# Raw weights of a half-size tile loaded in two halves with buffers of their own, and no sums issued behind the last plain tile

## The chip, the core and the metric

The kernel runs on one core of a Trainium2 chip. Such a core has TensorE (PE) for matmuls, VectorE (DVE), ScalarE (ACT), GpSimd (POOL) and SyncE (SP), each with its own stream of instructions, and 16 DMA engines that all queues share. Here SP issues the loads of weights and POOL issues transfers between two places in DRAM. The metric is the time of one execution in microseconds of device time.

## The reference

One layer of a streaming encoder over 512 positions of 1024 features, in float32: a half-weighted SwiGLU block (FFN1), a mixer (chunked attention beside a pooling mixer), another SwiGLU block (FFN2), and a last norm.

```python
D_MODEL = 1024
SEQ = 512
D_FF = 2816

def rmsnorm(x, g):
    xf = x.astype(jnp.float32)
    y = xf * lax.rsqrt(jnp.mean(xf * xf, axis=-1, keepdims=True) + EPS)
    return (y * g.astype(jnp.float32)).astype(x.dtype)

def swiglu_ffn(x, w_gate, w_up, w_down):
    return (jax.nn.silu(x @ w_gate) * (x @ w_up)) @ w_down

x = x + 0.5 * swiglu_ffn(rmsnorm(x, ffn1_norm[l]), ffn1_w_gate[l], ffn1_w_up[l], ffn1_w_down[l])
x = x + hybrid_mixer(rmsnorm(x, mix_norm[l]), w_in[l], q_norm[l], k_norm[l], rel_bias[l],
                     pool_w[l], pool_scale[l], w_out[l])
x = x + 0.5 * swiglu_ffn(rmsnorm(x, ffn2_norm[l]), ffn2_w_gate[l], ffn2_w_up[l], ffn2_w_down[l])
x = rmsnorm(x, final_norm[l])
```

The change touches the two SwiGLU blocks alone.

## The kernel before

**Precision.** Every float32 operand is split in two parts, a high one (a cast on ACT) and a low one (the raw value less the high part, on DVE). A product of two operands is three matmuls, high by high, low by high and high by low (lines 192 to 194). So a weight panel can be used once it is loaded ("raw"), cast (`whi`) and subtracted (`wlo`).

**The up stage of a SwiGLU block.** The 2816 hidden features are 22 tiles of 128. A tile has a gate and an up panel of 1024x128 weights, loaded as 128x1024. Tiles 0 and 1 run together in four steps; tiles 2, 3 and 4 are "plain" (`PLAIN = 5`): each panel is loaded, split and multiplied over 8 blocks of 128 rows by 512 columns. The 17 tiles from 5 on are "half-size": the products of gate and up are worked out from seven products of half the size (in Winograd's manner), each of 12 matmuls by 256 columns, from blocks of the weights and sums of blocks.

**A half-size tile's weights.** The two panels make four blocks of 512 columns: up low (called 11), gate low, gate high, up high. Block 11 is split by `high11` and `low11`, the last two together by `high(22)` and `low(22)`. `sum13` makes the sums 11 + gate low and gate low + gate high (1024 columns in one instruction), `sum24` makes two more from these, and `high13`, `low13`, `high24`, `low24` split the sums. All of this for tile n+1 is done while the products of tile n run. In the trace all splits of blocks are lines 490 (ACT) and 495 (DVE), `sum13` is line 513 and `sum24` lines 519 and 520; evacuations by ACT are line 587.

**Raw buffers.** The four blocks of a tile lie in one buffer of 128x2048, of which there are two. `fetch(n)` issues two loads of 512 KB on SP: line 482 (gate low and gate high) and line 483 (up low and up high). `fetch(n + 2)` is called in tile n behind its second product and waits for `low(22)` of tile n, the last reader of the buffer. Sums and the down stage's panels use other buffers of 128x1024 (pool `weights`, also called raw).

**The down stage.** 42 products, seven kinds for each of six groups of the hidden features; most have 12 matmuls of 512 columns. Kinds A11, A12, S1 to S4 and A22 of the activations meet weights B11 to B22 or the sums T1 to T4 of these. The sums are made in DRAM by POOL while the up stage runs: `make_sums` pops a number from the list `RATES`, and issues so many steps (line 724), each a copy or an accumulating copy of 512 KB, behind a small copy (`mark`, line 722) of something that was just computed, which sets their time. T1 to T4 of group g are two steps each (T3-4-1 is the second, accumulating step of T3, group 4). What isn't done by the end of the up stage follows in the first products of the down stage. The panels (line 748) are fetched a few products ahead, in buffers that cycle through a list called `rooms`.

**What sets the order.** In the half-size tiles the order of PE, DVE, ACT and SP is that of the code. In the plain tiles a scheduler sets it. POOL's order is that of the code in `make_sums`. In the down stage of FFN2, SP also issues loads of the residual (`xt`, line 810) and of the last norm's gain.

Of the kernel before, what the change touches and what calls it, by code (L numbers as in the profile page):

```python
# [8 lines left out]
F32 = mybir.dt.float32  # L9
# [3 lines left out]
ALU = mybir.AluOpType  # L13
# [3 lines left out]
P = 128  # L17
D = 1024
S = 512
KD = D // P  # L20
NT = S // P
FF = 2816
KF = FF // P
# [15 lines left out]
ROOM, AHEAD_OF_PARTS, ALIGN = 1024 + 128, 16, 64  # L39
OFF, OFF_AT = (0, 2, 6), 32  # L40
PLAIN = 5
RATES = [3, 3, 2] + [1] * (PLAIN - 3) + [2] * (FF // P - PLAIN - 2) + [0] * 2
PROBS = 3
M_TILES = 16

# [24 lines left out]
def layer(  # L70
# [47 lines left out]
    def name(what):  # L118
        n_tiles[0] += 1
        return f"{what}_{n_tiles[0]}"  # L120
# [307 lines left out]
    def ffn_up(norm, wA, down, loaded):  # L428
# [45 lines left out]

        raws, w = {}, {}

        def fetch(n):

            if n < KF:
                f = down.order[n]  # L480
                raw = raws[n] = down.pool.tile([P, 4 * S], F32, tag="raw", name=name("raw"), bufs=RAW)
                nc.sync.dma_start(raw[:, S : 3 * S], wA[2 * f])
                nc.sync.dma_start(
                    raw.rearrange("p (b c) -> p b c", c=S)[:, 0:4:3],
                    wA[2 * f + 1].rearrange("p (b c) -> p b c", c=S),
                )

        def high(n, what, src, at=AHEAD_OF_PARTS):
            hi, lo = (z[:, : src.shape[-1]] for z in part_tiles(at))
            nc.scalar.copy(hi, src)  # L490
            w[what] = hi, lo, src
# [8 lines left out]

        def high11(n):
            if n < KF:
                high(n, (n, 11), raws[n][:, :S])

        def low11(n):
            if n < KF:
# [2 lines left out]
        def sum13(n):  # L509
            if n < KF:  # L510
                z = w[n, "odd"] = new_sum()
                raw = raws[n]
                nc.vector.tensor_tensor(z, raw[:, : 2 * S], raw[:, S : 3 * S], op=ALU.add)  # L513

        def sum24(n):
            if n < KF:
                z = w[n, "even"] = new_sum()
                raw, odd = raws[n], w[n, "odd"]
                nc.vector.tensor_tensor(z[:, :S], odd[:, :S], raw[:, 2 * S : 3 * S], op=ALU.add)
                nc.vector.tensor_tensor(z[:, S:], z[:, :S], raw[:, 3 * S :], op=ALU.add)  # L520

        def high13(n):
            if n < KF:
                off = n - PLAIN in OFF
                high(n, (n, 13), w[n, "odd"], OFF_AT if off else AHEAD_OF_PARTS)
# [27 lines left out]
        n, f = PLAIN - 1, down.order[PLAIN - 1]  # L553
        wj = [weights(wA[2 * f + j]) for j in range(2)]
        banks = [bank(), bank()]
        fetch(PLAIN)
        for k in range(KD):
            for j in range(2):
                mm3(banks[j], cut(wj[j], k * P, P), norm.h[k], k == 0, k == KD - 1)
            if k == 1:  # L560
                high11(PLAIN)
                low11(PLAIN)
                piece()
            elif k == 3:
                fetch(PLAIN + 1)
                sum13(PLAIN)
                high13(PLAIN)
                low13(PLAIN)
                piece()
            elif k == 5:  # L570
                sum24(PLAIN)
                piece()
# [22 lines left out]
        with tc.manual_schedule(engines={E.PE, E.DVE, E.Activation, E.SP}):  # L595
            last_silu = last_place = last_sums = nothing
            for n in range(PLAIN, KF):
                f = down.order[n]
                acc, up_lo, up_hi = bank()[:, :HT], bank()[:, :HT], abank()[:, :HT]
                u, z, sg = temp(), temp(), temp()  # L600
                w11, w13, w24 = (w[n, i][:2] for i in (11, 13, 24))
                product(acc, w11, A11, True)
                last_silu()
                last_place()
                high(n, (n, 22), raws[n][:, 2 * S :])
                low((n, 22))
                w22 = w[n, 22][:2]
                copy(u[:, :HT], acc)
                product(up_hi, cut(w13, S, S), S3, True)
                if n + 2 < KF:  # L610
                    fetch(n + 2)
                elif n + 2 == KF:

                    rooms[:] = [(down.pool, "raw", RAW, 4 * S)] * RAW
                    rooms.extend([(wpool, "raw", RAW, 1024)] * RAW)
                    n_raw[0] = 0
                    down.fetch(T2, 0)
                else:
                    down.fetch(B11, 0)
                    down.fetch(T1, 0)  # L620
                high11(n + 1)
                low11(n + 1)
                if n + 1 == KF:
                    down.pairs[S2, 0] = down.tokens(S2, 0)
                last_sums()
                sum13(n + 1)
                copy(z[:, HT:], up_hi, -1.0)
                product(acc, cut(w24, 0, S), S2, False)
                copy(u[:, HT:], acc, -1.0)
                sum24(n + 1)  # L630
                product(up_hi, cut(w24, S, S), A22, False)
                nc.vector.tensor_tensor(u[:, HT:], up_hi, u[:, HT:], op=ALU.add)  # L632
                down.make_sums(u[:, HT:], 2)
                product(acc, cut(w13, 0, S), S1, False)
                copy(z[:, :HT], acc)
                nc.vector.tensor_tensor(z[:, HT:], z[:, :HT], z[:, HT:], op=ALU.add)
                if n + 1 == KF:
                    down.parts[T2, 0] = down.weights(T2, 0)
                    down.pairs[A11, 0] = down.tokens(A11, 0)
                high13(n + 1)  # L640
                low13(n + 1)
                high24(n + 1)
                product(up_lo, cut(w22, S, S), A12, True)
                nc.scalar.activation(sg[:, HT:], z[:, HT:], AF.Silu)
                nc.vector.tensor_tensor(u[:, :HT], up_lo, u[:, :HT], op=ALU.add)
                low24(n + 1)
                if n + 1 == KF:
                    down.parts[B11, 0] = down.weights(B11, 0)
                product(acc, cut(w22, 0, S), S4, False)

                def last_silu(acc=acc, sg=sg):
                    nc.scalar.activation(sg[:, :HT], acc, AF.Silu, scale=-1.0)

                def last_place(f=f, u=u, sg=sg):
                    down.place(f, u, sg)

                def last_sums(f=f):
                    down.sums(f)

            last_silu()  # L660
            last_place()
            last_sums()
# [4 lines left out]
    class Down:  # L667
# [37 lines left out]
        def begin(self, pool):  # L705
            self.pool, self.acts = pool, []
            self.raws, self.parts, self.pairs = {}, {}, {}
            self.n_products, self.loads, self.loads_from = 0, [], 4
            self.open(range(G - 3))
            rooms[:] = [(wpool, "raw", RAW, 1024), (pool, "raw", RAW, 4 * S)] * RAW  # L710
            part_rooms[:] = [(wpool, HILO)] * HILO + [(pool, 1)]

        def rows(self, i, g):
# [1019 lines left out]
```

## Time and profile before

| | |
|---|---|
| median of 3 runs | 841.92 us (841.59 to 842.51) |
| profiled execution | 840.54 us, of which span 838.6 us |
| granted TensorE clock | 0.998 |
| busy share of PE, DVE, ACT, POOL | 99%, 85%, 60%, 16% |
| moved by DMA | 158.50 MB, mean 189 GB/s |

A row of the timeline is start, duration (both us), engine, line, operation, output<-inputs, shape, count, and in brackets how long the engine idled before and what ended that. A row of the chain is start, duration, what. PE's instructions are pipelined, so its durations overlap; the distance from one start to the next tells more. FFN1's half-size tiles begin near 62 us, FFN2's near 560 us, and FFN2's down stage near 724 us. `raw<-in_wA_dram` are loads of the up stage's weights, `raw<-in_wB_dram` and `raw<-wsum` of the down stage's panels and sums, `wsum<-in_wB_dram` and `wsum<-wsum` POOL's steps for the sums.

### The profile page before, as it was taken

How to read it: one execution, taken by the hardware profiler on the slowest of the kernel's cores; microseconds unless marked ns; L12 is line 12 of the kernel's file. 1: busy time of each engine (PE TensorE's matmuls, PEld its weight loads, DVE VectorE, ACT ScalarE, POOL GpSimd, SP SyncE). 2: the span in 40 equal slices, each digit the busy share in tenths (PEclk: the TensorE clock that was granted, in tenths of full speed). 3: DMA queues.
4: the chain of work that ended last, by engine and by line, in shares of the span. 5: the costliest groups of instructions: out<-in, count | busy, mean ns of one | idle time of the engine just before them, and what ended most of it. 6: DMA issues, size and time to landing. Idle time of an engine off the chain costs nothing.

```text
span 838.6 us, 14134 instructions
## 1 busy us (share of the span) xinstructions
PE 828.4 (99%) x5288; PEld 742.3 (89%) x5288; DVE 710.9 (85%) x1122; ACT 501.5 (60%) x859; POOL 132.7 (16%) x208
## 2 busy tenths in 40 slices
PE   9999999999999999999999999999999999999996
PEld 7889999999988888887888888889999999978885
DVE  7999998999897769767879678979989999878896
ACT  8446555665675656558748646355566555756573
POOL 0222122211053000102020000311121111132000
PEclk9999999999999999999999999999999999999999
DMA  8687887797499964322222117658887787689832
GB/s 291 160 228 201 215 210 212 209 231 197 151 269 290 304 210 132 113 88 89 75 76 76 51 55 271 195 132 222 239 208 194 206 226 202 251 265 344 261 110 100
DMA packets 72244, 158.50 MB, mean 189 GB/s; under 512 B 6112, under 2 KB 29168, under 8 KB 71792
## 3 DMA queue, kind: packets, MB, share of 16 engines
q1 hardware_dynamic: 49088, 110.93, 38.8%
q0 software_dynamic: 22656, 46.14, 26.1%
q8 instruction: 41, 0.67, 0.3%
q10 hardware_dynamic: 432, 0.54, 0.2%
q14 instruction: 27, 0.22, 0.1%
HBM read 153.38 MB, written 50.34 MB: 243 GB/s over the span
## 4 chain that ended last, share of the span: by engine, by line
PE 93%; DMA 4%; DVE 2%; ACT 1%; issue 0%; SPq 0%; ACTq 0%; DVEq 0%
PE mm L192 22%; PE mm L194 22%; PE mm L193 22%; PE a L192 7%; PE a L194 7%; PE a L193 7%; DMA raw<-in_wA_dram 2%; DMA raw<-in_wB_dram 1%; PE a L1293 1%; PE a L1229 1%; PE a L1281 1%; DVE wlo L495 1%; PE a L229 0%; PE a L1500 0%; PE a L1151 0%; DVE ha L149 0%
## 5 line engine op out<-in xcount | busy, mean ns | idle before, releaser
L149 DVE TENSOR_TENSOR wlo<-raw,whi 128x1024 fp32r<-128x1024 f32 (+2 forms) x115 | 124.3, 1088 | 25.2 <-ACT whi L148 24.9
L148 ACT CAST whi<-raw 128x1024 fp32r<-128x1024 f32 (+2 forms) x115 | 107.7, 945 | 62.6 <-PE mm L193 17.0
L193 PE MATMUL mm<-ha,whi 128*128 128x256 f32 x408 | 112.8, 276 | 0.0
L192 PE MATMUL mm<-ha,whi 128*128 128x256 f32 x408 | 112.8, 276 | 0.0
L194 PE MATMUL mm<-ha,wlo 128*128 128x256 f32 x408 | 112.7, 276 | 0.0
L587 ACT ACTIVATE t<-mm 128x256 f32<-128x256 f32 x102 | 39.1, 384 | 114.2 <-PE mm L194 111.5
L495 DVE TENSOR_TENSOR wlo<-wsum,whi 128x1024 fp32r<-128x1024 f32 x68 | 82.9, 1220 | 9.8 <-PE mm L194 7.4
L193 PEld LDWEIGHTS mm<-ha,whi 128*128 128x128 f32 x408 | 76.6, 188 | 0.1
L192 PEld LDWEIGHTS mm<-ha,whi 128*128 128x128 f32 x408 | 76.6, 188 | 0.1
L194 PEld LDWEIGHTS mm<-ha,wlo 128*128 128x128 f32 x408 | 76.6, 188 | 0.0
L192 PE MATMUL mm<-hhi,whi 128*128 128x512 f32 x192 | 75.5, 396 | 0.0
L194 PE MATMUL mm<-hhi,wlo 128*128 128x512 f32 x192 | 74.8, 391 | 0.0
L193 PE MATMUL mm<-hlo,whi 128*128 128x512 f32 x192 | 74.7, 390 | 0.0
L722 POOL COPY mark<-t 128x1 f32<-128x1 f32 x44 | 15.0, 341 | 373.4 <-DVE t L632 236.5
L724 POOL DMA_DIRECT2D wsum<-in_wB_dram x72 | 70.6, 1069 | 10.0 <-issue 7.0
L193 PE MATMUL mm<-wlo,ah 128*128 128x512 f32 x176 | 68.6, 390 | 0.6 <-DVE wlo L149 0.6
L490 ACT CAST whi<-wsum 128x1024 fp32r<-128x1024 f32 x68 | 67.9, 1047 | 1.6 <-DVE wsum L513 1.4
L194 PE MATMUL mm<-whi,ah 128*128 128x512 f32 x176 | 68.5, 389 | 0.0
L495 DVE TENSOR_TENSOR wlo<-raw,whi 128x512 fp32r<-128x512 f32 x68 | 62.3, 950 | 7.2 <-ACT whi L490 7.2
L192 PE MATMUL mm<-whi,ah 128*128 128x512 f32 x176 | 68.4, 390 | 0.0
L490 ACT CAST whi<-raw 128x512 fp32r<-128x512 f32 x68 | 56.3, 828 | 11.8 <-PE mm L194 6.9
L192 PE MATMUL a<-whi,ah 128*128 128x512 f32 (+1 forms) x154 | 55.7, 362 | 0.0
(228 smaller groups left out, 2374.5 us busy)
## 6 DMA issues: line engine op xcount, KB each, us to landing
raw<-in_wA_dram SPq DMA_DIRECT2D x87, 512.0 KB, 5.6
wsum<-in_wB_dram POOLq DMA_DIRECT2D x60, 512.0 KB, 7.8
raw<-wsum SPq DMA_DIRECT2D x40, 512.0 KB, 4.7
raw<-in_wB_dram SPq DMA_DIRECT2D x30, 512.0 KB, 5.4
wsum<-wsum POOLq DMA_DIRECT2D x20, 512.0 KB, 5.3
x<-in_xT_dram SPq DMA_DIRECT2D x16, 256.0 KB, 6.6
raw<-in_wQK_dram SPq DMA_DIRECT2D x8, 512.0 KB, 3.5
raw<-in_wO_dram SPq DMA_DIRECT2D x8, 512.0 KB, 3.4
```

The costliest lines, as they stand in the source:

```text
L148: nc.scalar.copy(hi, src)
L149: nc.vector.tensor_tensor(lo, src, hi.bitcast(F32), op=ALU.subtract)
L192: nc.tensor.matmul(acc, a[0], b[0], start=start, stop=False, **more)
L193: nc.tensor.matmul(acc, a[0], b[1], start=False, stop=False, **more)
L194: nc.tensor.matmul(acc, a[1], b[0], start=False, stop=stop, **more)
L490: nc.scalar.copy(hi, src)
L495: nc.vector.tensor_tensor(lo, src, hi.bitcast(F32), op=ALU.subtract)
L587: nc.scalar.activation(dst, src, AF.Copy, scale=scale)
L722: nc.gpsimd.tensor_copy(mark, after[:, 0:1])
L724: nc.gpsimd.dma_start(self.rows(i, g), self.rows(self.terms[i][at], g), **(dict(accum_op=ALU.add) if at else {}),)
L1229: nc.tensor.matmul(banks[i][:, at : at + n], qT[pair][0][a][rows, t * P : (t + 1) * P], kT[pair][0][b][rows, :n], start=a + b == 0, stop=a ...
L1281: nc.tensor.transpose(tp[:, n : n + P], prob[h, t][:, j * P : (j + 1) * P], ident)
```

## The change

Each raw tile becomes two tiles of 128x1024 with buffers of their own, two of each: "ra" (block 11 and gate low) and "rb" (gate high and up high). The bytes are the same. Each half is two loads of 256 KB. `rb` of tile n+2 is fetched where the whole tile was, `ra` of tile n+3 is fetched in tile n behind `sum13(n + 1)`, which is the last reader of the buffer it takes. `sum13` becomes two instructions, since its inputs now lie in two buffers. The first fetches of the down stage move with it: T2-0 comes one tile sooner, B11-0, T1-0 and T2-1 spread over the last two tiles. `rooms` has four halves where it had two whole tiles. In `RATES` the plain part is 2, 2, 2, 2, 0 instead of 3, 3, 2, 1, 1.

```diff
-RATES = [3, 3, 2] + [1] * (PLAIN - 3) + [2] * (FF // P - PLAIN - 2) + [0] * 2
+RATES = [2] * (PLAIN - 1) + [0] + [2] * (FF // P - PLAIN - 2) + [0] * 2
...
-        def fetch(n):
+        def fetch(n, which):
 
             if n < KF:
                 f = down.order[n]
-                raw = raws[n] = down.pool.tile([P, 4 * S], F32, tag="raw", name=name("raw"), bufs=RAW)
-                nc.sync.dma_start(raw[:, S : 3 * S], wA[2 * f])
-                nc.sync.dma_start(
-                    raw.rearrange("p (b c) -> p b c", c=S)[:, 0:4:3],
-                    wA[2 * f + 1].rearrange("p (b c) -> p b c", c=S),
-                )
+                raw = raws[n, which] = down.pool.tile(
+                    [P, 2 * S], F32, tag=which, name=name("raw"), bufs=RAW
+                )
+                half = slice(0, S) if which == "ra" else slice(S, 2 * S)
+                for i, j in enumerate((1, 0) if which == "ra" else (0, 1)):
+                    nc.sync.dma_start(raw[:, i * S : (i + 1) * S], wA[2 * f + j][:, half])
...
         def sum13(n):
             if n < KF:
                 z = w[n, "odd"] = new_sum()
-                raw = raws[n]
-                nc.vector.tensor_tensor(z, raw[:, : 2 * S], raw[:, S : 3 * S], op=ALU.add)
+                a, b = raws[n, "ra"], raws[n, "rb"]
+                nc.vector.tensor_tensor(z[:, :S], a[:, :S], a[:, S:], op=ALU.add)
+                nc.vector.tensor_tensor(z[:, S:], a[:, S:], b[:, :S], op=ALU.add)
...
-        fetch(PLAIN)
+        fetch(PLAIN, "ra")
+        fetch(PLAIN, "rb")
...
-                fetch(PLAIN + 1)
+                fetch(PLAIN + 1, "ra")
+                fetch(PLAIN + 1, "rb")
                 sum13(PLAIN)
+                fetch(PLAIN + 2, "ra")
...
                 product(up_hi, cut(w13, S, S), S3, True)
                 if n + 2 < KF:
-                    fetch(n + 2)
+                    fetch(n + 2, "rb")
                 elif n + 2 == KF:
-
-                    rooms[:] = [(down.pool, "raw", RAW, 4 * S)] * RAW
-                    rooms.extend([(wpool, "raw", RAW, 1024)] * RAW)
-                    n_raw[0] = 0
-                    down.fetch(T2, 0)
+                    down.fetch(B11, 0)
                 else:
-                    down.fetch(B11, 0)
-                    down.fetch(T1, 0)
+                    down.fetch(T2, 1)
                 high11(n + 1)
                 low11(n + 1)
...
                 last_sums()
                 sum13(n + 1)
+                if n + 3 < KF:
+                    fetch(n + 3, "ra")
+                elif n + 3 == KF:
+                    rooms[:] = [(down.pool, tag, RAW, 2 * S) for tag in ("ra", "rb")] * RAW
+                    rooms.extend([(wpool, "raw", RAW, 1024)] * RAW)
+                    n_raw[0] = 0
+                    down.fetch(T2, 0)
+                elif n + 2 == KF:
+                    down.fetch(T1, 0)
```

PE's order is the same in both kernels. SP's order in FFN2 at the passage from plain to half-size tiles; before, the rows are the loads of plain panels (line 185: tile 2 up, tile 3 gate and up, tile 4 gate and up) and then the fetches of half-size tiles 5, 6 and 7:

```order
L185 DMA raw_6239<-in_wA_dram 128x1024
L185 DMA raw_6287<-in_wA_dram 128x1024
L185 DMA raw_6325<-in_wA_dram 128x1024
L185 DMA raw_6387<-in_wA_dram 128x1024
L185 DMA raw_6393<-in_wA_dram 128x1024
L482 DMA raw_6401<-in_wA_dram 128x1024
L483 DMA raw_6401<-in_wA_dram 128x2x512
L482 DMA raw_6440<-in_wA_dram 128x1024
L483 DMA raw_6440<-in_wA_dram 128x2x512
L482 DMA raw_6548<-in_wA_dram 128x1024
L483 DMA raw_6548<-in_wA_dram 128x2x512
```

and after, where the halves are line 486 and come as ra and rb of tile 5, ra and rb of tile 6, ra of tile 7, rb of tile 7, ra of tile 8:

```order
L185 DMA raw_6315<-in_wA_dram 128x1024
L185 DMA raw_6363<-in_wA_dram 128x1024
L185 DMA raw_6401<-in_wA_dram 128x1024
L185 DMA raw_6470<-in_wA_dram 128x1024
L486 DMA raw_6478<-in_wA_dram 128x512 x2
L185 DMA raw_6464<-in_wA_dram 128x1024
L486 DMA raw_6481<-in_wA_dram 128x512 x2
L486 DMA raw_6520<-in_wA_dram 128x512 x2
L486 DMA raw_6523<-in_wA_dram 128x512 x2
L486 DMA raw_6529<-in_wA_dram 128x512 x2
L486 DMA raw_6634<-in_wA_dram 128x512 x2
L486 DMA raw_6644<-in_wA_dram 128x512 x2
```

The first halves of tile 5 moved ahead of the last plain panel, and ra of tile 7 ahead of everything that tile 5 itself issues.

POOL's order at the start of FFN2's down stage; before, the marks of the last two up tiles without sums, and then the sums of the first products (T3-4-1 and T4-2-1, both accumulating, and the copy T4-4-0):

```order
L722 COPY mark_8569<-t_8493 128x1
L722 COPY mark_8695<-t_8623 128x1
L722 COPY mark_8903<-ah_8895 128x1
L724 DMA wsum_152<-in_wB_dram 256x1x512
L722 COPY mark_8956<-ah_8949 128x1
L724 DMA wsum_156<-in_wB_dram 256x1x512
L722 COPY mark_9010<-ah_9002 128x1
L724 DMA wsum_158<-wsum_146 16x8192
```

and after (T3-5-0, of half the size and not accumulating, the copy T4-3-0, then T3-4-1 and T4-2-1):

```order
L732 COPY mark_8717<-t_8638 128x1
L732 COPY mark_8841<-t_8771 128x1
L732 COPY mark_9047<-ah_9039 128x1
L734 DMA wsum_153<-in_wB_dram 128x512
L732 COPY mark_9100<-ah_9093 128x1
L734 DMA wsum_157<-wsum_145 16x8192
L732 COPY mark_9154<-ah_9146 128x1
L734 DMA wsum_152<-in_wB_dram 256x1x512
L732 COPY mark_9208<-ah_9200 128x1
L734 DMA wsum_156<-in_wB_dram 256x1x512
```

The two accumulating sums moved two marks back.

More of the change, by code (lines that the diff above doesn't have):

```diff
@@ L502, in high11 @@
             if n < KF:
-                high(n, (n, 11), raws[n][:, :S])
+                high(n, (n, 11), raws[n, "ra"][:, :S])
         def low11(n):
@@ L517, in sum24 @@
                 z = w[n, "even"] = new_sum()
-                raw, odd = raws[n], w[n, "odd"]
-                nc.vector.tensor_tensor(z[:, :S], odd[:, :S], raw[:, 2 * S : 3 * S], op=ALU.add)
-                nc.vector.tensor_tensor(z[:, S:], z[:, :S], raw[:, 3 * S :], op=ALU.add)
+                raw, odd = raws[n, "rb"], w[n, "odd"]
+                nc.vector.tensor_tensor(z[:, :S], odd[:, :S], raw[:, :S], op=ALU.add)
+                nc.vector.tensor_tensor(z[:, S:], z[:, :S], raw[:, S:], op=ALU.add)
         def high13(n):
@@ L604, in ffn_up @@
                 last_place()
-                high(n, (n, 22), raws[n][:, 2 * S :])
+                high(n, (n, 22), raws[n, "rb"])
                 low((n, 22))
@@ L709, in begin @@
             self.open(range(G - 3))
-            rooms[:] = [(wpool, "raw", RAW, 1024), (pool, "raw", RAW, 4 * S)] * RAW
+            rooms[:] = [
+                z for tag in ("ra", "rb") for z in ((wpool, "raw", RAW, 1024), (pool, tag, RAW, 2 * S))
+            ]
             part_rooms[:] = [(wpool, HILO)] * HILO + [(pool, 1)]
```

## The prediction

> **What bounds the kernel now.** I read the page first: shares of busy time, then the engines along the chain that ended last.
>
> ```profile
> span 838.6 us, 14134 instructions
> PE 828.4 (99%) x5288; PEld 742.3 (89%) x5288; DVE 710.9 (85%) x1122; ACT 501.5 (60%) x859; POOL 132.7 (16%) x208
> PE 93%; DMA 4%; DVE 2%; ACT 1%; issue 0%; SPq 0%; ACTq 0%; DVEq 0%
> ```
>
> TensorE is the bound, and the order of its instructions is the same in both kernels. So the change can win only where TensorE stands still for a late operand, and can lose only by making it stand still in new places. Of the chain, 4% is DMA: those are places where a load was late. The view of waits says little on them, since it lists only gaps that leave PE idle by its modelled ends, so I went through PE's rows and took the distance from one start to the next: 0.11 us for 256 columns, 0.23 us for 512. Behind the first 25 us it is exceeded by over 0.2 us in four places in the stages the change touches. The largest:
>
> ```profile
> 574.50 0.28 PE L194 MATMUL mm<-xa,wlo 128*128 128x256 f32 x1
> 576.01 0.39 PE L192 MATMUL a<-ha,whi 128*128 128x256 f32 x1 [1.23 <-ACT t L587]
> 576.23 0.28 PE L193 MATMUL a<-ha,whi 128*128 128x256 f32 x1
> 565.11 0.34 SPq L482
> 565.49 9.48 DMA raw<-in_wA_dram
> 575.05 0.62 ACT whi L490
> ```
>
> Starts 574.50 and 576.01 are 1.51 us apart instead of 0.11, and the next pair 0.22: lost 1.40 + 0.11 = 1.51 us. The wait is put down to ACT's row L587, but the chain (the last three lines) says what was late: the second load of raw tile 7 (block 11, the first thing needed, is in it) was issued at 565.49 and took 9.48 us; `high11(7)` started at 575.05, and the two copies that free the PSUM banks stand behind it on ACT. The load could not leave earlier, because its buffer was freed by `low22(5)`.
>
> The same place in the first FFN:
>
> ```profile
> 75.18 0.28 PE L193 MATMUL mm<-xa,whi 128*128 128x256 f32 x1
> 75.29 0.28 PE L194 MATMUL mm<-xa,wlo 128*128 128x256 f32 x1
> 75.70 0.39 PE L192 MATMUL a<-ha,whi 128*128 128x256 f32 x1
> 75.92 0.28 PE L193 MATMUL a<-ha,whi 128*128 128x256 f32 x1
> 66.09 8.58 DMA raw<-in_wA_dram
> 74.74 0.62 ACT L490 CAST whi<-raw 128x512 fp32r<-128x512 f32 x1 [1.47 <-DMA raw<-in_wA_dram]
> ```
>
> 0.41 - 0.11 = 0.30 and 0.22 - 0.11 = 0.11: 0.41 us, by the same load of raw tile 7.
>
> The third is in FFN2's first half-size tile, and its cause lies 13 us earlier:
>
> ```profile
> 563.20 0.28 PE L194 MATMUL a<-xa,wlo 128*128 128x256 f32 x1
> 563.55 0.38 PE L192 MATMUL mm<-xa,whi 128*128 128x256 f32 x1
> 563.77 0.29 PE L193 MATMUL mm<-xa,whi 128*128 128x256 f32 x1
> 537.78 0.33 SPq L482 DMA_DIRECT2D raw<-in_wA_dram  x1
> 550.50 0.69 DVE L495 TENSOR_TENSOR wlo<-raw,whi 128x512 fp32r<-128x512 f32 x1 [4.62 <-ACT whi L490]
> 551.00:561.00 10.00, 10.00 (x48) 8.37 (x47) 9.93 (x17) 6.25 (x11) 1.93 (x3) 1.00 0.55 126
> 561.00:571.00 10.00, 9.93 (x86) 9.73 (x86) 9.93 (x16) 6.27 (x12) 3.42 (x5) 1.00 0.48 123
> ```
>
> 0.35 - 0.11 = 0.24 and 0.22 - 0.11 = 0.11: 0.35 us. Raw tile 5 is fetched only at 537.78, so VectorE idles 4.62 us before `low11(5)` at 550.50 and is then full for 20 us (the two stretches: 9.93 of 10 busy; columns are sum, PE, PE loads, DVE, ACT, POOL). Behind that backlog everything is late.
>
> The fourth is in FFN2's down products:
>
> ```profile
> 751.90 0.39 PE L192 MATMUL mm<-whi,ah 128*128 128x512 f32 x1
> 752.90 0.50 PE L193 MATMUL mm<-wlo,ah 128*128 128x512 f32 x1 [0.60 <-DVE wlo L149]
> 753.23 0.39 PE L194 MATMUL mm<-whi,ah 128*128 128x512 f32 x1
> 738.87 11.59 DMA raw<-in_wB_dram
> 750.53 1.05 ACT L148 CAST whi<-raw 128x1024 fp32r<-128x1024 f32 x1 [4.45 <-DMA raw<-in_wB_dram]
> 752.37 1.05 ACT L148 CAST whi<-raw 128x1024 fp32r<-128x1024 f32 x1 [0.27 <-DMA raw<-wsum]
> 735.96 1.05 POOL L724 DMA_DIRECT2D wsum<-in_wB_dram  x1
> 736.68 2.18 POOL L724 DMA_DIRECT2D wsum<-in_wB_dram  x1
> 744.17 0.38 SPq L748 DMA_DIRECT2D raw<-wsum  x1
> ```
>
> 1.00 - 0.23 = 0.77 and 0.33 - 0.23 = 0.10: 0.87 us. The load of B11-3 left at 738.87 and took 11.59 us; POOL's queue had got two accumulating 512 KB sums 2 to 3 us earlier.
>
> Together 1.51 + 0.41 + 0.35 + 0.87 = 3.14 us. That is all the change can regain by these rows.
>
> **The change, part by part.** *Halves with own buffers.* The first half ("ra": blocks 11 and lower gate) of tile n+3 is issued after `sum13(n+1)` in tile n, one tile before its old place (7 products of 12 matmuls at 0.113 us, 9.5 us); for raw tile 7 that is behind `sum13(5)`, which in FFN2 follows the row at 550.50, so near 552 instead of 565. It then has over 20 us to `high11(7)`. Both waits for raw 7 go: -1.51 and -0.41. The second half ("rb") stays behind `low22(n)`, and is needed by the new second piece of `sum13(n+2)`; the old one shows when:
>
> ```profile
> 577.11 1.22 DVE L513 TENSOR_TENSOR wsum<-raw 128x1024 f32<-128x1024 f32 x1
> 566.20 1.22 DVE L513 TENSOR_TENSOR wsum<-raw 128x1024 f32<-128x1024 f32 x1
> 567.45 0.69 DVE L519 TENSOR_TENSOR wsum<-wsum,raw 128x512 f32<-128x512 f32 x1
> 557.32 3.69 DVE L149 TENSOR_TENSOR ha<-aside,ha 128x512 fp32r<-128x512 f32 x6
> ```
>
> From 565.11 to 577.11 + 0.6 are 12.6 us; the longest load on the chain took 11.59. It should hold, with less in front: the two lower blocks alone, and no sum issued behind the last plain tile.
>
> *Raw tile 5 sooner.* In SP's order its halves now stand between the loads of the last plain tile and wait for buffers that the plain tiles' splits free. A plain panel is 8 x 3 matmuls at 0.227 us, 5.4 us, and `rb(5)` now waits for the split of tile 2's up panel, at least two panels before the one it waited for; so it leaves some 11 us or more before 537.78 (an estimate), and 4.62 us are needed. `low11(5)` loses its 4.62 us wait, DVE's work starts early, and the 0.35 us goes: -0.35.
>
> *SP.* Four issues a tile rather than two. An issue takes 0.34 us (565.11), so 0.7 us more a tile on a queue that issues twice in 9.5 us. What is queued behind are only the next halves. Where a half waits for its buffer, all later loads of SP wait too; in the up stage these are nothing but halves. Nothing on the path.
>
> *DVE.* `sum13` becomes two instructions of 128x512. Six such take 3.69 us, 0.60 each by distance, so 1.20 against 1.22 + 0.03 (567.45 - 566.20 = 1.25). The bound upwards is 2 x 0.69 = 1.38, so +0.13 us in 34 tiles at most. In a steady tile DVE has that to spare:
>
> ```profile
> 88.86 0.43 DVE L636 TENSOR_TENSOR t<-t 128x256 f32<-128x256 f32 x1 [0.82 <-ACT t L587]
> 89.73 1.23 DVE L495 TENSOR_TENSOR wlo<-wsum,whi 128x1024 fp32r<-128x1024 f32 x1 [0.44 <-PE mm L194]
> ```
>
> 0.82 + 0.44 = 1.26 us idle in one tile, of which 0.13 is covered ten times over. If that cover were gone, it would cost at most 34 x 0.13 = 4.4 us. I take 0.
>
> *Rates and the sums.* From the last plain tile on the sums run two steps later than before. Their last uses lie many products behind. At the start of FFN2's down stage, where the two accumulations at 735.96 and 736.68 starved B11-3, the queue now gets a plain 256 KB copy (T3-5-0) and the plain copy T4-3-0, and the accumulations come two products later each, near 742 and 747. Bounds of this term: B11-3's stall goes wholly, -0.87; or the next load, T1-3, takes its place. Its cast at 752.37 also waited for its load, and with 750.53 -> 752.90 as the way from cast to matmul (2.37 us) it is ready at 754.74; one product is 12 x 0.227 = 2.72 us, so without the stall it is needed near 752.13 + 2.72 = 754.85. Slack 0.1 us: if T1-3 lands no sooner, -0.87 still holds; if it takes 11.59 us as B11-3 did, it lands 3.4 us later (issue 744.17, landing just ahead of 752.37 before; 744.17 + 11.59 = 755.76) and the term is +2.5. I take -0.87, nearer to the old row, because the traffic ahead of T1-3 is smaller by an accumulation.
>
> *Rooms.* The down stage's loads cycle through 10 buffers in FFN2 rather than 8; SP's order there is bound by `xt` loads that wait for PE (738.50 just ahead of B11-3's issue), so they leave no sooner. 0. T2-0 is fetched a tile sooner, 0.
>
> Sum: -1.51 - 0.41 - 0.35 - 0.87 = -3.14 us. Profiled execution 840.54 (1.94 around the span) -> 837.4; it stands 1.38 below the median, so against the median 841.92: 838.8.
>
> A rule against the change: the Trainium skill, "DMA: Bandwidth & Descriptors", section "Measured (HBM→SBUF, 128 partitions, SWDGE, issued from GpSimd)", says to batch transfers to 1 MiB or more for three quarters of the peak, and the fit in "Anatomy of one DMA — SWDGE (gpsimd) path" charges about 2 us fixed for each. An estimate by that fit, 2.6 us for each of four quarters of the tile, is 10.4 us in a 9.5 us tile if nothing overlapped: +0.9 us a tile. The rows below speak for overlap; halved loads are the last rival.
>
> **The rivals.** (a) All four waits go: 838.8. (b) The raw waits go, the down stage's stays in size at the next load: 841.92 - 2.27 = 839.7. (c) Raw tile 7 is late at another operand (rb, or VectorE's backlog that moves rather than goes): half the raw gain and the down wait kept, 840.8. For it: DMA's share is high exactly there; against it: the 12.6 us window. (d) T1-3 takes 11.59 us: +2.5 - 2.27 = 842.2, no change. (e) Slower: the halves do not overlap.
>
> ```profile
> x_d<-t SPq DMA_DIRECT2D x8, 256.0 KB, 3.1
> raw<-in_wO_dram SPq DMA_DIRECT2D x8, 512.0 KB, 3.4
> 504.67 4.99 SPq L1505 DMA_DIRECT2D x_d<-t  x8
> ```
>
> 256 KB take 3.1 us where 512 KB take 3.4. Four in a row without overlap would be 12.4 us a tile, 2.9 over the tile's 9.5, in 30 steady tiles +87 us: about 929. It decides from 9.5 us for four, 2.4 each. Against it: eight such were issued in 4.99 us, 0.62 apart, at 3.1 us each, so five were under way at once. A milder form, every rb 1 us later than its need in five tiles, gives 843.8. That the change does nothing at the waits (the halves queued behind each other as before) is (c) at its end.
>
> **How the numbers follow.** Chances: (a) 0.48, (b) 0.24, (c) 0.12, (d) 0.08, (e) 0.08. About 0.2% or 1.7 us is what a measurement tells from no change. (a), (b) and half of what (c) spreads over are faster: 0.78; the other half of (c) and (d) no change: 0.14; (e) slower: 0.08. Time: 838.8. Low: (a) less the 0.9 us between the three runs of before, 837.9. High: it takes in (b) and the middle of (c), 841.0, and leaves out (d) and (e), 0.16.
>
> **What would show it.** In the changed trace PE's distances at 75.3, 563.2, 574.5 and 751.9 (all shifted by what was regained before) are 0.11 and 0.23; `high11(7)` has no DMA as releaser; DVE's row before `low11(5)` idles under 1 us; `sum13`'s two pieces take 1.2 us, the second not released by a DMA; casts of B11-3 and T1-3 start before 750. It is wrong if a DMA releases DVE's second piece of `sum13` tile after tile, if the chain's DMA share stays at 4%, or if POOL's accumulations near 742 to 750 leave T1-3 or T2-4 late.

## The result, and the profile after

The changed kernel takes 838.41 us (median of 4 runs, 837.33 to 838.59) against 842.21 us (4 runs, 841.59 to 842.77) for the kernel before: a ratio of 0.9952, with a 95% interval of 0.9935 to 0.997. The forecast was 838.8, in a range of 837.9 to 841.0. In all sets of runs together the kernel before was timed 67 times: 66 times lie between 838.46 and 847.39 us, and one of 1693.86 us, in a slow state, is left out of the ratios.

The page of the changed kernel, the lines that answer to the first three of before:

```profile
span 836.7 us, 14334 instructions
PE 827.8 (99%) x5288; PEld 742.3 (89%) x5288; DVE 711.1 (85%) x1156; ACT 501.7 (60%) x859; POOL 153.1 (18%) x212
PE 97%; DMA 1%; DVE 1%; SPq 0%; ACT 0%; issue 0%; DVEq 0%; ACTq 0%
```

DMA's share of the chain fell from 4% to 1%; the kernel's 34 additional VectorE instructions cost 0.2 us of busy time in all. At the four places of the prediction PE no longer waits. The passage at 574 in FFN2 (PE's timeline, start and duration in us), then the passage at 751 in the down stage:

```profile
574.48 0.28 PE L194 MATMUL mm<-xa,wlo 128*128 128x256 f32 x1
574.60 0.28 PE L192 MATMUL a<-ha,whi 128*128 128x256 f32 x1
574.71 0.28 PE L193 MATMUL a<-ha,whi 128*128 128x256 f32 x1
...
750.31 0.39 PE L192 MATMUL mm<-whi,ah 128*128 128x512 f32 x1
750.53 0.39 PE L193 MATMUL mm<-wlo,ah 128*128 128x512 f32 x1
```

Starts are 0.12 and 0.11 us apart where 1.51 and 0.22 stood, and 0.22 where 1.00 stood. But the profiled spans differ by 1.9 us only, not by 3.1. Three things gave some back. The first matmuls waited 0.4 us longer for the first loads; by the measure explained below, the first 25 us lose 1.1 to 2.5 us in the profiles of this case. A new wait stands in FFN1's down stage:

```profile
282.95 0.39 PE L192 MATMUL a<-whi,ah 128*128 128x512 f32 x1
283.33 0.50 PE L193 MATMUL a<-wlo,ah 128*128 128x512 f32 x1
283.67 0.40 PE L194 MATMUL a<-whi,ah 128*128 128x512 f32 x1
```

(0.38 and 0.34 us instead of 0.23: lost 0.15 + 0.11, and with a smaller one before it 0.4 to 0.5 us.) And the tail behind the last matmul grew from 7.3 to 7.9 us, of which 0.4 us is one gap on VectorE that nothing shown explains. The same gap stands in the profiles of the three kernels below that keep the halves as two loads each and change only rates or fetches; with whole raw tiles, or with one load per half, it is absent and the tail is 7.3 to 7.4 us (with 4 and 8 buffers it is absent too, and the tail 7.6). So it goes with the program and not with the execution. The chain of the changed kernel there:

```profile
829.46 0.02 DVEq L1552
829.48 0.41 issue
829.89 0.16 DVE u L1552
```

and the same place before:

```profile
831.96 0.02 DVEq L1542
831.98 0.04 issue
832.02 0.16 DVE u L1542
```

### The profile page after: what moved, and what is told of

The parts are those of the page before. It is cut to its first block, busy times and chain, and to the rows that moved or that the text cites. A ratio compares the mean times of both kernels' runs of the same rounds, so it can differ in the third digit from the quotient of the medians.

```text
span 836.7 us, 14334 instructions
## 1 busy us (share of the span) xinstructions
PE 827.8 (99%) x5288; PEld 742.3 (89%) x5288; DVE 711.1 (85%) x1156; ACT 501.7 (60%) x859; POOL 153.1 (18%) x212
## 4 chain that ended last, share of the span: by engine, by line
PE 97%; DMA 1%; DVE 1%; SPq 0%; ACT 0%; issue 0%; DVEq 0%; ACTq 0%
PE mm L192 23%; PE mm L193 23%; PE mm L194 23%; PE a L193 8%; PE a L192 8%; PE a L194 8%; PE a L1303 1%; PE a L1239 1%; PE a L1291 1%; DMA raw<-in_wA_dram 1%; PE a L1510 0%; PE a L1161 0%; PE a L309 0%; PE a L894 0%; PE mm L894 0%; SPq L185 0%
## 5 line engine op out<-in xcount | busy, mean ns | idle before, releaser
L732 POOL COPY mark<-t 128x1 f32<-128x1 f32 x44 | 17.5, 398 | 392.8 <-DVE t L640 242.5
```

The source lines that it names most:

```text
L732: nc.gpsimd.tensor_copy(mark, after[:, 0:1])
```

## The experiments

Since time tells half a microsecond badly, the experiments are read by PE's rows: all kernels have the same 5288 matmuls in the same order, so for each place the loss is the sum of the distances from start to start, less the least distance that any of the profiles shows for the same pair. "Up stage" is the sum of the three places at 75, 563 and 574; "272" is the stretch from 272 to 284 in FFN1's down stage, "752" the one in FFN2's. All in us, one profiled execution each; the median is of all timed runs (in brackets: a single run).

| kernel | at 75 | at 563 | at 574 | up stage | 272 | 752 | median |
|---|---|---|---|---|---|---|---|
| before, the profile of the prediction | 0.42 | 0.37 | 1.54 | 2.33 | 0.10 | 0.93 | 842.21 |
| before, second profile | 0.01 | 0.02 | 0.46 | 0.49 | 2.07 | 1.38 | (841.63) |
| before, third profile | 0.01 | 0.02 | 0.63 | 0.66 | 1.54 | 0.58 | (840.46) |
| changed | 0.01 | 0.02 | 0.02 | 0.05 | 0.52 | 0.03 | 838.41 |
| changed, old rates | 0.01 | 0.02 | 0.02 | 0.05 | 0.10 | 0.63 | 839.1 |
| before, new rates | 0.01 | 0.02 | 0.02 | 0.05 | 2.42 | 0.03 | 840.7 |
| changed, first half not early | 0.01 | 0.02 | 0.02 | 0.05 | 0.47 | 0.03 | 838.5 |
| changed, not early, old rates | 0.01 | 0.02 | 0.02 | 0.05 | 0.10 | 0.03 | 839.1 |
| changed, down buffers 4 and 8 | 0.01 | 0.02 | 0.02 | 0.05 | 2.28 | 0.03 | 840.21 |
| changed, one load per half | 0.01 | 0.02 | 0.02 | 0.05 | 0.17 | 0.03 | 838.43 |
| before, loads swapped | 0.01 | 0.02 | 0.02 | 0.05 | 1.67 | 1.28 | 840.43 |
| changed, mark on ACT | 0.01 | 0.02 | 0.02 | 0.05 | 0.10 | 0.03 | 838.16 |
| before, mark on ACT | 0.64 | 0.02 | 0.66 | 1.32 | 1.31 | 0.03 | 839.56 |
| before, swap and mark | 0.01 | 0.02 | 0.02 | 0.05 | 2.05 | 0.03 | 839.07 |

The kernel before was run along with each set, with medians of 842.21, 841.68, 842.5 and 842.35. The ratios to it were:

| kernel | ratio | 95% interval |
|---|---|---|
| changed | 0.9952 | 0.9935 to 0.997 |
| changed, old rates | 0.9968 | 0.9951 to 0.9984 |
| before, new rates | 0.9984 | 0.9969 to 0.9999 |
| changed, first half not early | 0.995 | 0.9932 to 0.9969 |
| changed, not early, old rates | 0.9963 | 0.9952 to 0.9975 |
| changed, down buffers 4 and 8 | 0.9984 | 0.9968 to 0.9999 |
| changed, one load per half | 0.9953 | 0.9938 to 0.9969 |
| before, loads swapped | 0.9972 | 0.996 to 0.9985 |
| changed, mark on ACT | 0.9948 | 0.9929 to 0.9967 |
| before, mark on ACT | 0.9972 | 0.9959 to 0.9985 |
| before, swap and mark | 0.9967 | 0.9951 to 0.9984 |

### Halves or rates: the two parts apart

The changed kernel with the old rates:

```diff
-RATES = [2] * (PLAIN - 1) + [0] + [2] * (FF // P - PLAIN - 2) + [0] * 2
+RATES = [3, 3, 2] + [1] * (PLAIN - 3) + [2] * (FF // P - PLAIN - 2) + [0] * 2
```

> The changed kernel with the RATES of before, so the halves and their early fetch alone. Theory H (the early first half ends the waits for raw tile 7, the early fetch of tile 5 ends the wait at 563, the shifted sums end the wait at 752): PE's extra distances at 75, 563 and 574 us are under 0.1 us, the one in FFN2's 11th down product is back at 0.5 to 0.9 us; 839.0 to 839.6 us. Rival R (raw tile 7 was late only because sums stood in front of it behind the last plain tile): 0.4 us at 75 and 1.5 us at 574 are back, about 841.

The forecast of theory H held: no wait in the up stage, 0.63 us back at the 11th down product, 839.1 us. (Its reason, the early first half, is tested further down.) Its PE timeline there:

```profile
750.13 0.39 PE L192 MATMUL mm<-whi,ah 128*128 128x512 f32 x1
750.83 0.50 PE L193 MATMUL mm<-wlo,ah 128*128 128x512 f32 x1 [0.31 <-DVE wlo L149]
```

The kernel before with the new rates (the same line the other way round):

> The kernel before with the new RATES alone: no sum behind the last plain tile, sums two steps later, raw tiles whole. H: waits of at least 0.2 us at 75, 0.3 at 563 and 0.8 at 574 stay, since the load still leaves at 65 and 565; the one at 752 goes; 840.3 to 841.3. R: those at 75 and 574 go, 563 stays; 838.6 to 839.6.

Here the theory fell, and the rival was right for 75 and 574: with whole raw tiles, none early, these waits are gone. The one at 563, which both expected to stay, is gone as well. The load that was late shows why. The loads of raw tile 7 by the view of the raw tiles from 564 to 568, before:

```profile
L483 SPq DMA_DIRECT2D raw<-in_wA_dram x1: 551/551/551, 565.5 to 565.5; - x1
DMA to landing us min/median/max: 3.6/6.5/9.5
```

and with the new rates alone:

```profile
L483 SPq DMA_DIRECT2D raw<-in_wA_dram x1: 551/551/551, 567.4 to 567.4; - x1
DMA to landing us min/median/max: 3.5/4.0/4.5
```

The second load is issued no earlier, but takes 4.5 us rather than 9.5. Before, POOL's accumulating sum had left 0.04 us ahead of the pair at 565.11:

```profile
565.07 1.03 POOL L724 DMA_DIRECT2D wsum<-in_wB_dram  x1
```

In return, the kernel with the new rates waits 2.42 us at 272 in FFN1's down stage, and 0.6 us more than the others at 764 in FFN2's, so it ended at 840.7, within the forecast of the theory it disproved.

### Does the early first half do anything?

```diff
                 if n + 2 < KF:
+                    fetch(n + 2, "ra")
                     fetch(n + 2, "rb")
...
-                if n + 3 < KF:
-                    fetch(n + 3, "ra")
-                elif n + 3 == KF:
+                if n + 3 == KF:
```

(and the same for tile 7 in the last plain tile.)

> The changed kernel, but the first half of tile n+2 is fetched with its second half at the old place in tile n, so that it has half a tile's less time; buffers, halves and rates as in the change. H: the first half of tile 7 leaves near 565 instead of 548 in FFN2, a wait of 0.2 to 1.2 us comes back at 574, that of tile 5 stays gone; 838.6 to 840. R: nothing comes back, 838.4, since no sum stands in front.

838.5 us, and PE's rows are those of the changed kernel within 0.2 us from the first tile to the last. The early load is worth nothing here beside the new rates. With the old ones, where a sum does stand in front:

> The fourth corner of the square of rates and early fetch: halves, the first one not early, RATES of before, so that sums again stand in front of raw tile 7's loads. The runs so far: the new rates alone ended the waits at 75, 563 and 574, and the early first half added nothing beside them. Theory E (with sums in front, the early half is what ends the wait): 0.2 to 0.4 us at 75 and 0.5 to 1.5 us at 574 are back, 840 to 841. Theory B (block 11, needed first, stood in the second load before and in the first now, and the first of a pair lands in 3.5 us at any rate): nothing comes back in the up stage, 839.1 as with the early half.

Theory B held: nothing came back in the up stage, 839.1 as with the early half. Three of tile 7's four loads of 256 KB fall in the window from 564 to 568, with the sum 0.05 us in front (565.38); the trace has a landing for two of them, those of the first half, block 11 among them, and they took 2.7 and 3.5 us:

```profile
L486 SPq DMA_DIRECT2D raw<-in_wA_dram x3: 327/328/441, 565.4 to 567.9; - x3
DMA to landing us min/median/max: 2.7/3.1/3.5
```

The fourth, of the second half, was issued at 568.24 and took 6.5 us; `sum24(7)`, the first that needs it, came at 577.56 and did not wait. So the two loads issued first land soon, not all of them.

(The wait at 752 did not come back in this execution, though the rates were the old ones and it is there in the five other profiles with the old rates and POOL's own mark. Nothing here explains that.)

The order of the two loads alone, in the kernel before:

```diff
-                nc.sync.dma_start(raw[:, S : 3 * S], wA[2 * f])
                 nc.sync.dma_start(
                     raw.rearrange("p (b c) -> p b c", c=S)[:, 0:4:3],
                     wA[2 * f + 1].rearrange("p (b c) -> p b c", c=S),
                 )
+                nc.sync.dma_start(raw[:, S : 3 * S], wA[2 * f])
```

> The kernel before with the two loads of a raw tile in the other order (the one with block 11 first), nothing else. B: the waits at 75 and 574 go (-1.9), those at 563 and 752 stay; 839.4 to 840.2. E: the loads run side by side and land together near 575, the wait at 574 stays at 1.0 to 1.5; 841.0 to 842.

The up stage's waits went, with the sum in front and whole tiles: block 11 is in the first load, which landed in 4.6 us, and the second one's 7.9 us are early enough for `sum13` (the least and the longest of the view of raw tiles in that window):

```profile
DMA to landing us min/median/max: 4.6/6.3/7.9
```


Two statements in another order do for raw tile 7 what the new buffers were meant to do. The wait at 563, which was to stay, is absent too. Even so, the time, 840.43, is above the forecast: 272 lost 1.67 us, which the forecast did not have, beside the 1.28 at 752, which it had.

### One load per half

```diff
-                for i, j in enumerate((1, 0) if which == "ra" else (0, 1)):
-                    nc.sync.dma_start(raw[:, i * S : (i + 1) * S], wA[2 * f + j][:, half])
+                nc.sync.dma_start(
+                    raw.rearrange("p (j c) -> p j c", c=S),
+                    wA[2 * f : 2 * f + 2, :, half].rearrange("j p c -> p j c"),
+                )
```

> The changed kernel with each half as one load of 512 KB (128x2x512) instead of two of 256 KB; the order of the two blocks inside ra is changed with it. If the size of a load matters at this traffic, the larger loads win: 0.3 to 1 us less, or shorter landings by over 0.5 us. I expect no change beyond 0.2 us in PE's distances: no load of a half ends a wait in the changed kernel.

838.43 against 838.41 us. The groups of DMA issues, the changed kernel and then this one (count, size, median us to landing):

```profile
raw<-in_wA_dram SPq DMA_DIRECT2D x136, 256.0 KB, 4.0
```

```profile
raw<-in_wA_dram SPq DMA_DIRECT2D x87, 512.0 KB, 4.8
```

(The 87 loads include the 19 of plain panels, which have 512 KB in both kernels.) Half the size lands 0.8 us sooner, not in half the time, but the loads of a tile overlap, so nothing is lost. Of PE's distances, 272 alone changed by more than the 0.2 us expected (0.17 against 0.52), and the tail is 0.6 us shorter in this profile; the medians show neither. The rule of the Trainium skill that the prediction weighed ("DMA: Bandwidth & Descriptors", section "Measured (HBM→SBUF, 128 partitions, SWDGE, issued from GpSimd)") would charge for the split. It was measured on transfers issued from GpSimd, and these are issued by SP; the two medians differ by 0.02 us, so this kernel shows no such charge.

### The new wait at 272, and what hides it

The down stage's buffers as deep as before:

```diff
                     rooms[:] = [(down.pool, tag, RAW, 2 * S) for tag in ("ra", "rb")] * RAW
-                    rooms.extend([(wpool, "raw", RAW, 1024)] * RAW)
```

> The changed kernel with the down stage's buffers as deep as before (4 in FFN1, 8 in FFN2, rather than 6 and 10). The changed kernel has a new wait of 0.4 us at 282, in FFN1's down stage, behind a 128x1 copy on POOL that took 11.78 us (0.18 elsewhere) and five sums issued within 8 us of its end. Theory D (the deeper buffers keep VectorE busy without a pause, POOL's copy gets through only in a pause): the copy ends at 245 or before as in the kernel before, the sums spread, the wait at 282 goes, time -0.4. Rival: the wait comes from the later sums alone and stays at 0.3 to 0.5.

Theory D was wrong twice: POOL's copy takes just as long (11.76 us), and the wait does not go but grows from 0.52 to 2.28 us, the time to 840.21; the rival had it stay. PE's waits in this kernel:

```profile
276.21 0.50 PE L193 MATMUL mm<-wlo,ah 128*128 128x512 f32 x1 [0.76 <-DVE wlo L149]
...
279.66 0.50 PE L193 MATMUL a<-wlo,ah 128*128 128x512 f32 x1 [0.43 <-DVE wlo L149]
```

So the two additional buffers, a by-product of cutting the raw region in four, are worth 1.8 us at this place. That made the first trace of the kernel before suspect, which has 4 buffers and no wait there. It was profiled twice more.

> The kernel before, profiled once more. Its first profiled execution took 840.54, below all its other runs of that day (841.59 to 842.77), and it is the only trace so far in which POOL's first copy in FFN1's down stage took 1.25 us; with the swapped loads the same place had 11.26 us, a burst of sums and 1.4 us of waits at 275 to 282. Theory M: the kernel before mostly has that burst too; the copy takes 11 us here and PE waits 1 to 1.5 us at 275 to 282, or the times of the two go together. Rival: 1.25 us again, no wait there.

> The same once more, for the spread: M expects 11 us in at least one of the two.

Theory M held in both: POOL's copy took 11.81 and 11.78 us, and 2.07 and 1.54 us are lost, somewhat more than the 1 to 1.5 expected. PE's waits at 272 in the second profile:

```profile
275.47 0.50 PE L193 MATMUL mm<-wlo,ah 128*128 128x512 f32 x1 [0.57 <-DVE wlo L149]
...
281.98 0.50 PE L193 MATMUL mm<-wlo,ah 128*128 128x512 f32 x1 [0.58 <-DVE wlo L149]
```

In these two profiles the kernel before loses 1.5 to 2.1 us there, and only 0.5 to 0.7 in the up stage. The chain of the second profile still goes through the second load of raw tile 7, which took 8.56 us rather than 9.48:

```profile
566.44 0.34 SPq L482
...
566.82 8.56 DMA raw<-in_wA_dram
...
575.46 0.62 ACT whi L490
```

Over all profiles with 4 buffers in FFN1's down stage the loss at 272 is 0.10, 2.07, 1.54, 2.42, 2.28, 1.67, 1.31 and 2.05 us; over those with 6 it is 0.52, 0.10, 0.47, 0.10, 0.17 and 0.10. Seven of the eight with 4 buffers lose 1.3 us or more, none of the six with 6 more than 0.52. In this stretch DMA is full; the row of 262 to 272 in the second profile (sum, PE, PE loads, DVE, ACT, POOL, clock, DMA share, GB/s) has a DMA share of 1.13:

```profile
262.00:272.00 10.00, 10.00 (x45) 8.28 (x45) 7.33 (x10) 4.63 (x7) 1.15 (x1) 1.00 1.13 285
```

Why the first profile of the kernel before had no wait there isn't settled; its DMA share in the same stretch is no lower, 1.16.

### POOL's mark

```diff
+            if down:
+                mark = small.tile([P, 1], F32, tag="mark", name=name("mark"))
+                nc.scalar.copy(mark, after[:, 0:1])
+                seen = dram.tile([1, 1], F32, name=name("seen"))
             with tc.manual_schedule(engines={mybir.EngineType.Pool}):
-                mark = small.tile([P, 1], F32, tag="mark", name=name("mark"))
-                nc.gpsimd.tensor_copy(mark, after[:, 0:1])
+                if down:
+                    nc.gpsimd.dma_start(seen, mark[0:1])
+                else:
+                    mark = small.tile([P, 1], F32, tag="mark", name=name("mark"))
+                    nc.gpsimd.tensor_copy(mark, after[:, 0:1])
```

> The changed kernel, in which the down stage's mark is copied by ACT, and POOL's queue waits for it with a transfer of 4 bytes instead of a copy of its own. Theory L (POOL's copy cannot reach SBUF while VectorE runs without a pause, hence 11.78 us for 128x1): the sums leave one by one from 235 on, no burst at 246 to 254, the load of T1 that took 16.5 us takes under 11, and the wait of 0.4 us at 282 goes; 838.0. Rival: POOL is late for what it waits for (ACT's cast), then the first sum still leaves at 246 and the wait stays.

The forecast of theory L held. In the changed kernel POOL's timeline has

```profile
234.91 11.78 POOL L732 COPY mark<-ah 128x1 f32<-128x1 f32 x1 [13.69 <-ACT ah L148]
246.64 0.75 POOL L734 DMA_DIRECT2D wsum<-in_wB_dram  x1
```

and with the mark on ACT

```profile
236.55 0.55 POOL L737 DMA_DIRECT2D seen<-mark  x1 [15.62 <-ACT mark L733]
237.07 0.80 POOL L742 DMA_DIRECT2D wsum<-in_wB_dram  x1
239.97 0.52 POOL L737 DMA_DIRECT2D seen<-mark  x1 [2.10 <-ACT mark L733]
```

The first sum leaves 9.6 us sooner, the sums are spread, the load of a sum issued at 264 takes 9.8 us rather than 16.5, and the wait of 0.52 us is gone. That the burst makes this wait isn't shown, though: with one load per half the copy took 11.78 us, the same burst followed, that load took 16.0 us, and PE lost only 0.17 us; the two profiles with 6 buffers and the old rates have the copy of 11.81 us and lose 0.10. At 838.16 us (4 runs, 838.03 to 838.59) this is the fastest kernel of the study by its median, though not by more than the runs scatter.

The same edit in the kernel before:

> The kernel before with the mark of the down stage copied by ACT, so that POOL's queue waits by a transfer of 4 bytes; nothing else. M: no burst, no wait at 275 to 282, the waits at 75, 563 and 574 stay (2.3 us); that at 752 goes or moves, since the sums leave some 5 us sooner; 840.0 to 840.6. Rival: as before, 841.5 to 842.5.

The forecast of 840.0 to 840.6 was too slow by 0.4 us (839.56; the profiled execution took 840.27), and two of its terms were wrong. The wait at 752 went, as expected: the sums leave sooner. But the up stage waits 1.32 us rather than 2.3, with nothing at 563, and at 272 PE still waits 1.31 us, with no burst at all. With 4 buffers the wait comes without the burst; of the edits made here, only the two more buffers made it small.

> The kernel before with the loads of a raw tile swapped and the mark on ACT: no halves, no new buffers, RATES of before. If the waits are all there is to the change's gain, and each is ended by these two small edits, the time is that of the changed kernel within 0.4 us, 838.0 to 838.9; if the new buffers do something else, 839.5 or more.

839.07 us, between the two forecasts. Up stage and 752 are clean, 272 keeps 2.05 us. By PE's rows, what the new buffers add over these two small edits is the depth in FFN1's down stage. The medians are only 0.7 us apart, and these 5 runs go from 837.73 to 840.95 us, so the time alone does not show it.

## Why the prediction was right, point by point

**The bound.** "TensorE is the bound" held: the gain is made of waits that PE no longer has, and apart from the start, the stretch at 272 and the tail nothing else moved by more than 0.1 us.

**Raw tile 7, -1.51 and -0.41.** Both waits went, but the step named the wrong part of the change. It said that the half a tile's earlier issue ends them. The runs show that this is not needed: without it nothing comes back, with the new rates or with the old. No sum in front is enough by itself, and so is block 11 in the first load of the pair. The change holds three remedies for one wait. Each of the four profiles without any of them loses 0.46 to 1.54 us at 574, each of the other ten 0.02. Whether the third, the early issue, would be enough by itself isn't shown: with the halves block 11 always stands in the first loads. The line "The load could not leave earlier, because its buffer was freed by `low22(5)`" was true, but an earlier issue was not the only way to an earlier landing; the row of POOL's sum at 565.07, which was not read there, was the other half. The size was that of one execution as well: in two more profiles of the kernel before the wait at 574 is 0.46 and 0.63, and there is none at 75.

**Raw tile 5, -0.35.** `low11(5)` now runs without a pause, in a row of VectorE's timeline that has no idle time in brackets:

```profile
546.14 0.68 DVE L495 TENSOR_TENSOR wlo<-raw,whi 128x512 fp32r<-128x512 f32 x1
```

The halves were issued at 517 to 521, over 16 us before 537.78, as the step said (11 us or more), and the wait at 563 is gone. It is gone, too, in the six other profiles with the old fetch of tile 5, two of them of the kernel before itself, so it was not there to be gained in most executions. The step's cause, "fetched only at 537.78", was half of it: in these six the loads leave as late (539 to 541). In the first profile the load with block 11 took 11.6 us. In the four of the six with the old order of loads it took 5.6 to 8.4 us, and VectorE idled 1.42 us or less ahead of `low11(5)`, in the third profile of the kernel before this long:

```profile
547.81 0.69 DVE L495 TENSOR_TENSOR wlo<-raw,whi 128x512 fp32r<-128x512 f32 x1 [0.50 <-ACT whi L490]
```

**The down product at 752, -0.87.** Right in mechanism, and in size for the execution it was read from. The casts of B11-3 and T1-3 start before 750, as the prediction said; the first no longer waits for its load, the second still does, by 0.51 us, which PE does not feel:

```profile
744.39 1.03 ACT L148 CAST whi<-raw 128x1024 fp32r<-128x1024 f32 x1
749.02 1.05 ACT L148 CAST whi<-raw 128x1024 fp32r<-128x1024 f32 x1 [0.51 <-DMA raw<-wsum]
```

In all six kernels with the new rates the loss is 0.03 us; in six with the old rates and POOL's mark it is 0.93, 1.38, 0.58, 0.63, 1.28 and once 0.03. The next load, T1-3, did not take its place. With whole tiles and the new rates 0.6 us turned up at 764, behind a later load (close to rival b), in the changed kernel nothing.

**VectorE and SP at nothing.** Right. Each piece of `sum13` takes 0.69 us and starts 0.60 behind the one before; in all 34 tiles VectorE never idled ahead of either:

```profile
565.97 0.69 DVE L513 TENSOR_TENSOR wsum<-raw 128x512 f32<-128x512 f32 x1
566.57 0.69 DVE L514 TENSOR_TENSOR wsum<-raw,raw 128x512 f32<-128x512 f32 x1
567.17 0.68 DVE L520 TENSOR_TENSOR wsum<-wsum,raw 128x512 f32<-128x512 f32 x1
```

**Rooms, 0.** Wrong, and the largest error: the two more buffers are worth 1.8 us in FFN1's down stage. The step looked at FFN2 alone, where SP's `xt` loads hold the queue back, and at a trace that showed no wait in FFN1.

**The sum.** -3.14 was forecast, and -3.8 came out between the medians. The agreement is partly by chance: 3.14 were the waits of one execution, with little at 272. The other two profiles of before lose less in the up stage and 1.5 to 2.1 us at 272; all places together they lose 3.9 and 2.8 us, the first one 3.4. The changed kernel loses 0.6 there, and 0.6 more in its tail. That leaves 1.6 to 2.7 us; between the profiled executions (840.54, 841.63 and 840.46 against 838.57) the difference is 1.9 to 3.1. The rest up to 3.8 is that most of the kernel before's other executions are slower than its profiled ones, and for those there is no trace: that stays open.

## What to carry to other kernels

Before a wait for a load is cured by an earlier issue, look at what else is in the queues while it is under way, and which of the loads issued together is needed first: here both were free to change, and each was enough. A place where nothing waits in one profile can wait 2 us in the next, so where DMA is full a second profile of the unchanged kernel is worth more than a finer reading of the first. A by-product of a change (here two more buffers downstream) needs a term of its own in every stage that uses it.

## What the runs showed of the hardware

A copy of 128x1 on POOL took 0.18 us where VectorE had pauses, and 11.78 us beside VectorE instructions that follow each other without one. It ends when VectorE first idles. In the second profile of the kernel before:

```profile
234.78 11.81 POOL L722 COPY mark<-ah 128x1 f32<-128x1 f32 x1 [13.66 <-ACT ah L148]
```

```profile
245.87 0.68 DVE L149 TENSOR_TENSOR ah<-acts,ah 128x512 fp32r<-128x512 f32 x1
247.54 1.23 DVE L149 TENSOR_TENSOR wlo<-raw,whi 128x1024 fp32r<-128x1024 f32 x1 [1.00 <-ACT whi L148]
```

VectorE's instruction ends at 246.55, POOL's copy at 246.59, and everything queued behind it on POOL, five sums, leaves in a burst. So it is with all 27 such copies of over 4 us in these profiles: each ends 0.04 to 0.05 us behind the start of a pause of VectorE, and the copies of 5 us in FFN2's down stage behind pauses of 0.03 to 0.04 us. Not every copy needs a pause: in the first profile of the kernel before one took 1.25 us (from 235.86), though VectorE's rows show none before 245.03, and many copies of 1 to 3 us elsewhere have none either. The transfers that POOL issues were not held up in this way: with the mark on ACT they left at 237 to 244, while VectorE was busy all the time (10.00 of 10 us, behind length, PE and PE's loads):

```profile
235.00:245.00 10.00, 10.00 (x46) 8.29 (x45) 10.00 (x14) 7.43 (x13) 4.03 (x6) 1.00 0.94 307
```

The Trainium skill, "SBUF — State Buffer", section "SBUF: two separate sides", says that VectorE and GpSimd share a pair of ports by an exclusive lock, which a VectorE instruction with two SBUF inputs holds against a GpSimd instruction that reads SBUF. The long copies agree with it, and add the 11.8 us: instructions in close sequence can leave no opening for a copy. That the lock is the reason is argued, not shown, since no run changed VectorE's instructions, and the copy of 1.25 us stays unexplained.
